# A tuned two-layer mixer kernel: larger input stages, no value products in between, and grouped rank products

## The chip, the cores and the metric

One core of one Trainium2 chip runs the kernel. The metric is the device time of one execution in microseconds; lower is better. A profile comes from one profiled execution.

## The reference

A model of two layers works on 256 tokens `x` and 256 context tokens `ctx`, each of width 2048, in float32. Cut to what matters here, the first layer begins with

```python
sh, sc, gt = modulation(c, w_ada[0], b_ada[0], 3)        # silu(c) @ w_ada + b_ada, in three parts
u  = x * (1.0 + sc) + sh
uc = ctx * (1.0 + sc_c) + sh_c                           # with the modulation of c_ctx
k, v, rf, rb, q, gate_b, a_b, a_c, a_x, gate_a = split_cols(u @ w_in_e, E_SIZES)
# the context needs k, v and the gate ranks rf, rb alone
```

Keys and values are 1024 columns each, and the ranks `rf` and `rb` 16 each. Gated linear attention, a short convolution branch, an output projection and a layer norm follow. The second layer pools, multiplies by a gate and projects. The gate vector `gt` of both layers and the scale and shift of the second come from `w_ada` as well.

## The kernel before, in words

All weights are fp32 and are read once. A weight tile is split on the chip into a rounded high part (`wh`, a cast on ScalarE, line 153) and a remainder (`wl`, a subtraction on VectorE, line 154). The modulated input is split in the same way. A product is then three matmuls: high by high, high by remainder and remainder by high (`mm3`, lines 189 to 193). Products of 128 tokens with 512 columns accumulate over the contraction tiles in a PSUM bank; there are 16 contraction tiles of 128 channels.

The first stretch of the kernel makes the modulated input `u` and the keys together, in stages over the contraction tiles. `STAGES` (line 58) lists how many tiles each stage has: 1, 1 and then seven stages of 2. For a stage of n tiles, `stage_u` (line 362)

- loads the tiles of `x` and `ctx` (`load_xc`, line 208);
- multiplies silu of the conditioning vectors with the scale and shift columns of these n tiles, over the whole contraction of `w_ada` (`mod_rows`, line 264). The weights come as 1 MiB loads, each n * 128 columns wide; four contraction tiles are summed side by side in four groups of 32 partitions (line 275);
- turns the sums into per-channel columns (`to_cols`, line 284: a copy to `arow`, then matmuls to `adaT`), adds the biases, transposes the input tiles (`px`, lines 386 and 387), applies scale and shift, and splits the result;
- when a quad of four tiles is complete, multiplies it with the 32 rank columns of the weights (`pr`, line 402).

`stage_k` (line 411) then multiplies the n tiles with two blocks of 512 key columns for four token tiles, and adds the sums to `knat` (line 420 for the first stage, line 422 for later ones). In the loop at line 563 the program first calls `w_ahead`, which issues loads and splits of the previous stage's key weights, then `stage_u` of this stage, then `stage_k` of the previous one. After the keys of 2, 4, 6 and 8 tiles, `FILLS` (line 40) adds a part of the values: `v_fill` (line 439) multiplies two contraction tiles with value columns 0 to 511 for four token tiles. The partial sums go to `vnat` (lines 451 and 453). Their split weights lie in general slots (`swh`, `swl`).

The framework schedules each engine's instructions by a model of their durations, with the program's order (shifted by `prio`) as the priority; on the chip each engine then works through its list in order. All weight loads are issued on SP's queue (line 139) in order. They take turns in four raw buffers of 1 MiB each, shared by modulation weights and all other weights, and the split parts take turns in four `wh` and four `wl` buffers of two contraction tiles each. Four PSUM banks serve the accumulations and four all else.

After the keys, 32 transposes turn them round (`nT`, line 681). The values follow, two blocks of 512 columns in units of four contraction tiles (lines 762 to 776), where `V_Q` leaves out the quads that the fills have done. Behind each unit `tick` issues some background work: the decays of the attention, and steps of the remaining modulation sums on VectorE (`aacc`, line 530), three steps a unit in this block. The other blocks of the first layer, the output projection and the second layer come after that and are not touched.

Of the kernel before, what the change touches and what calls it, by code (L numbers as in the profile page):

```python
# [9 lines left out]
F32 = mybir.dt.float32  # L10
# [3 lines left out]
ALU = mybir.AluOpType  # L14
# [3 lines left out]
P = 128  # L18
# [5 lines left out]
EPS = 1e-5  # L24
# [8 lines left out]
ADA_0 = {}  # L33
# [7 lines left out]
FILLS = {2: [(0, 0, 2)], 4: [(0, 2, 2)], 6: [(0, 4, 2)], 8: [(0, 6, 2)]}  # L41
FILL_PRIO = 0
# [15 lines left out]
STAGES = (1, 1, 2, 2, 2, 2, 2, 2, 2)  # L58
# [3 lines left out]
def kernel(  # L62
# [96 lines left out]
    # units in the order of their use; loads and splits run ahead of the products  # L159
# [71 lines left out]
    # columns 2, 3: silu of c and c_ctx; a window of 32 columns puts them on the rows 0, 1 or 2, 3 of a product  # L231
# [5 lines left out]
    # columns of colT: see the rows above  # L237
# [26 lines left out]
    def mod_rows(k0, n):  # L264
        """scale (rows 0, 1 of each group of 32) and shift (rows 2, 3) of n channel tiles, summed over every fourth contraction tile"""
        nw = n * P
        ps = mp([P, nw], "ada")
        nk = 2048 // nw
        for half, c0 in ((0, D + k0 * P), (1, k0 * P)):
            for kk in range(0, KT, nk):  # L270
                r = load_unit(w_ada[0], kk, nk, c0, nw)
                for j in range(nk):
                    kt = kk + j
                    g = kt % 4
                    nc.tensor.matmul(  # L275
                        out=ps[32 * g : 32 * g + 32, :], lhsT=sil[:, kt, 2 - 2 * half : 34 - 2 * half], rhs=r[:, j, :],
                        start=half == 0 and kt < 4, stop=half == 1 and kt >= KT - 4,
                    )
        return ps
# [38 lines left out]
    for n in STAGES:  # L318
        for nb in range(2):
            specs.append((W_E, k0, n, nb * 512))  # L320
        k0 += n
        for nb, kt, nk in FILLS.get(k0, ()):
            specs.append((W_E, kt, nk, 1024 + nb * 512))
            wide.add(len(specs) - 1)
# [10 lines left out]

    filled = [[kt + j for f in FILLS.values() for nb, kt, nk in f if nb == n for j in range(nk)] for n in range(2)]
    V_Q = [[q for q in range(4) if 4 * q not in filled[n]] for n in range(2)]
    for nb in range(2):
        block(W_E, 1024 + nb * 512, V_Q[nb])
# [22 lines left out]
    def stage_u(k0, n):  # L362
        w, n0 = n * P, k0 * P
        xc = xcs.pop(k0, None)
        if xc is None:
            xc = load_xc(k0, n)
        xs, cs = xc[:, 0:2, :], xc[:, 2:4, :]
# [11 lines left out]
        for j in range(n):  # L379
            kt = k0 + j  # L380
            if kt % 2 == 0:
                quad_u.append(slot([P, 2, 512], F32, "u"))
            u = quad_u[-1]
            px = mp([P, 512], "px")
            for t in range(2):
                nc.tensor.transpose(out=px[:, t * P : (t + 1) * P], in_=xs[:, t, j * P : (j + 1) * P], identity=ident)
                nc.tensor.transpose(out=px[:, 256 + t * P : 256 + (t + 1) * P], in_=cs[:, t, j * P : (j + 1) * P], identity=ident)
            ux, uc = u[:, kt % 2, 0:256], u[:, kt % 2, 256:512]
            nc.scalar.activation(ux, px[:, 0:256], AF.Identity, bias=shT[:, kt, 0:1], scale=scT[:, kt, 0:1])
            nc.vector.tensor_scalar(  # L390
                out=uc, in0=px[:, 256:512], scalar1=scT[:, kt, 1:2], scalar2=shT[:, kt, 1:2], op0=ALU.mult, op1=ALU.add
            )
            q, i = kt // 4, kt % 4
            nc.scalar.copy(uxh[q][:, i, :], ux)
            nc.scalar.copy(uch[q][:, i, :], uc)
            nc.vector.tensor_tensor(out=uxl[q][:, i, :], in0=ux, in1=uxh[q][:, i, :].bitcast(F32), op=ALU.subtract)
            nc.vector.tensor_tensor(out=ucl[q][:, i, :], in0=uc, in1=uch[q][:, i, :].bitcast(F32), op=ALU.subtract)
            if i == 3:
                pr = mp([P, 512], "pr")
                for g in range(4):  # L400
                    kk = kt - 3 + g
                    nc.tensor.matmul(  # L402
                        out=pr[32 * g : 32 * g + 32, :], lhsT=wr[:, kk, :], rhs=quad_u[kk // 2][:, kk % 2, :],
                        start=True, stop=True,
                    )
                if q == 0:
                    nc.vector.tensor_copy(r_acc, pr)
                else:
                    nc.vector.tensor_tensor(out=r_acc, in0=pr, in1=r_acc, op=ALU.add)
# [27 lines left out]
    vnat = []  # L437

    def v_fill(nb, kt, nk):
        """a part of the values' contraction, for the gaps that the loads leave"""  # L440
        parts = w_next((W_E, kt, nk, 1024 + nb * 512), 0, 0)
        if not vnat:
            vnat.extend(slot([P, 1024], F32, "vnat") for _ in range(4))
        with prio(FILL_PRIO):
            for m in range(4):
                acc = acc_bank("vfill")
                for j in range(nk):
                    mm3(acc, utile(m, kt + j), parts[j], j == 0, j == nk - 1)
                dst = vnat[m][:, nb * 512 : (nb + 1) * 512]
                if kt == filled[nb][0]:  # L450
                    nc.scalar.copy(dst, acc)
                else:
                    nc.vector.tensor_tensor(out=dst, in0=acc, in1=dst, op=ALU.add)

# [20 lines left out]
    def ada_unit(layer, k0, n0):  # L475
        """four contraction tiles of the modulation's weights, two slots of two"""
# [26 lines left out]
    def ada_rows_gen(layer, dst, engs):  # L503
        """the gate of a layer, on every partition: products on DVE, the sum over the channels with ones"""
# [27 lines left out]
    def ada_cols_gen(layer, n0, dst, bias, one, engs, on_pe=()):  # L532
        """a section as channel columns: products on DVE, or on PE for the column blocks in on_pe"""
# [29 lines left out]
    for n in STAGES:  # L563
        if prev:
            w_ahead(2, SPLIT_0)
        stage_u(k0, n)
        if prev:
            stage_k(*prev)
            pump_ada(ADA_0.get(sum(prev), 0))
            for f in FILLS.get(sum(prev), ()):  # L570
                v_fill(*f)
        elif SPLIT_0:
            with tc.issue_after(arow_ins[0].ins):
                w_ahead(2, 2)
        prev = (k0, n)
        k0 += n
# [45 lines left out]
    def gemm_by_tile(groups, getu, done, budget=0.0, between=None, halves=False):  # L622
        """one token tile behind the other: the first one's sums are done while the second is at work"""
# [21 lines left out]
    # masks over (key j, query i) of a block of 32: m <= (j xor i) < 2 m  # L645
# [28 lines left out]
    def to_channels(nat, dst, use_act):  # L674
        """nat: two token tiles with 128 * n columns; dst(ct) for pairs of channel tiles"""
# [88 lines left out]
    if not vnat:  # L764
        vnat.extend(slot([P, 1024], F32, "vnat") for _ in range(4))
    gg = gate_gen()
    bg.append(gg)
    for nb in range(2):
        accs = [acc_bank("vacc") for _ in range(4)]
        gemm(W_E, 1024 + nb * 512, V_Q[nb], range(4), utile, accs, budget=B_V)  # L770
        for m in range(4):
            dst = vnat[m][:, nb * 512 : (nb + 1) * 512]
            if len(V_Q[nb]) < 4:
                nc.vector.tensor_tensor(out=dst, in0=accs[m], in1=dst, op=ALU.add)
            else:
                nc.scalar.copy(dst, accs[m])
# [21 lines left out]
    def gla_gen(hp):  # L798
# [19 lines left out]
        def scores(xk, xq, flip=0):  # L818
            """keys of a block of 32 against the queries of the same block, or of its neighbour"""
# [52 lines left out]
        # chunk of 64 against the next one, tile of 128 against the other  # L872
# [108 lines left out]
    def rsqrt_act(v):  # L981
        """1 / sqrt(v + EPS): logarithm and exponential, then a Newton step"""
# [8 lines left out]
    def rsqrt(v, scale):  # L991
        """1 / sqrt(scale * v + EPS) on DVE: a seed from the exponent bits, then Newton steps"""
# [75 lines left out]
    def ln_blocks(src, order, getu, res, gt, budget, after, before=None, between=None, halves=False):  # L1068
        """sums of residual and projection and their statistics; after(m, tiles, mean, variance) when token tile m is done"""
# [265 lines left out]
```

## Time and profile before

| | |
|---|---|
| time, median of 3 runs | 1018.31 us (1013.9, 1018.31 and 1018.49) |
| profiled execution, span | 1014.8 us (no other time of this execution is listed) |
| TensorE (PE) busy | 973.4 us, 96% of the span |
| VectorE (DVE) busy | 801.4 us, 79% |
| ScalarE (ACT) busy | 463.3 us, 46% |
| DMA moved | 255.45 MB, mean 252 GB/s |

The span is what the profiler recorded from the first to the last instruction. Matmuls are pipelined: one starts while the one before is still draining, so start times tell more than durations, and a busy share near 100% doesn't mean that PE was at its peak. In tables by window, PE, PEld (weight loads into PE), DVE, ACT and POOL show their busy microseconds and the number of instructions; then come the granted PE clock, the busy share of the DMA engines and the rate.

### The profile page before, as it was taken

How to read it: one execution, taken by the hardware profiler on the slowest of the kernel's cores; microseconds unless marked ns; L12 is line 12 of the kernel's file. 1: busy time of each engine (PE TensorE's matmuls, PEld its weight loads, DVE VectorE, ACT ScalarE, POOL GpSimd, SP SyncE). 2: the span in 40 equal slices, each digit the busy share in tenths (PEclk: the TensorE clock that was granted, in tenths of full speed). 3: DMA queues.
4: the chain of work that ended last, by engine and by line, in shares of the span. 5: the costliest groups of instructions: out<-in, count | busy, mean ns of one | idle time of the engine just before them, and what ended most of it. 6: DMA issues, size and time to landing. Idle time of an engine off the chain costs nothing.

```text
span 1014.8 us, 14425 instructions
## 1 busy us (share of the span) xinstructions
PE 973.4 (96%) x5718; PEld 768.6 (76%) x5718; DVE 801.4 (79%) x1161; ACT 463.3 (46%) x629; POOL 24.0 (2%) x55
## 2 busy tenths in 40 slices
PE   5899999999999999989999999999999999999995
PEld 4566666778878877877878788887888887778885
DVE  1555556989996999699999879987769968576676
ACT  2422214365684775336563444446554454454340
POOL 2000000000000000000000000000100001000000
PEclk9999999999999999999999999999999999999998
DMA  9987899667786676757767897984887888877532
GB/s 264 327 264 261 284 289 331 203 226 254 249 298 243 199 258 219 258 171 249 245 213 248 290 322 253 323 315 170 292 308 233 277 267 277 284 268 257 175 121 83
DMA packets 150373, 255.45 MB, mean 252 GB/s; under 512 B 5079, under 2 KB 46721, under 8 KB 150305
## 3 DMA queue, kind: packets, MB, share of 16 engines
q1 hardware_dynamic: 146592, 245.13, 72.3%
q0 software_dynamic: 2896, 8.72, 2.7%
q8 instruction: 45, 0.74, 0.3%
q10 hardware_dynamic: 816, 0.68, 0.3%
q14 instruction: 24, 0.19, 0.0%
HBM read 252.41 MB, written 2.10 MB: 251 GB/s over the span
## 4 chain that ended last, share of the span: by engine, by line
PE 43%; DVE 31%; DMA 19%; issue 4%; ACT 3%; SPq 0%; DVEq 0%; ACTq 0%
DMA raw<-in_w_ada_dram 16%; DVE wl L154 11%; DVE aacc L530 8%; PE oacc L191 5%; PE oacc L193 5%; PE oacc L192 5%; PE xacc L193 4%; PE xacc L192 4%; PE xacc L191 4%; PE ada L275 2%; PE kacc L191 2%; PE kacc L193 2%; PE kacc L192 2%; PE pr L402 1%; DMA raw<-in_w_in_e_dram 1%
## 5 line engine op out<-in xcount | busy, mean ns | idle before, releaser
L153 ACT CAST wh<-raw 128x1024 fp32r<-128x1024 f32 (+1 forms) x250 | 257.8, 1044 | 252.6 <-PE xacc L193 97.8
L154 DVE TENSOR_TENSOR wl<-raw,wh 128x1024 fp32r<-128x1024 f32 (+1 forms) x250 | 297.9, 1211 | 40.6 <-ACT wh L153 38.1
L530 DVE SCALAR_TENSOR_TENSOR aacc<-raw,sil,aacc 128x512 f32<-128x512 f32 x240 | 179.5, 748 | 42.6 <-DMA raw<-in_w_ada_dram 38.7
L191 PE MATMUL xacc<-wh,uxh 128*128 128x512 f32 x384 | 152.6, 397 | 0.0
L193 PE MATMUL xacc<-wh,uxl 128*128 128x512 f32 x384 | 151.8, 395 | 0.0
L192 PE MATMUL xacc<-wl,uxh 128*128 128x512 f32 x384 | 150.3, 391 | 0.1
L192 PE MATMUL xacc<-wl,u1h 128*128 128x512 f32 x240 | 94.4, 393 | 3.2 <-DVE wl L154 3.0
L191 PE MATMUL xacc<-wh,u1h 128*128 128x512 f32 x240 | 95.2, 397 | 0.8 <-ACT u1h L1156 0.8
L193 PE MATMUL xacc<-wh,u1l 128*128 128x512 f32 x240 | 93.7, 391 | 0.0
L192 PEld LDWEIGHTS xacc<-wl,uxh 128*128 128x128 f32 x384 | 72.1, 188 | 16.2 <-DVE wl L154 1.0
L193 PEld LDWEIGHTS xacc<-wh,uxl 128*128 128x128 f32 x384 | 72.2, 188 | 15.3 <-issue 0.2
L191 PEld LDWEIGHTS xacc<-wh,uxh 128*128 128x128 f32 x384 | 72.1, 188 | 15.5 <-ACT wh L153 0.5
L422 DVE TENSOR_TENSOR knat<-kacc,knat 128x512 f32<-128x512 f32 x64 | 42.8, 686 | 34.5 <-PE kacc L193 34.3
L192 PEld LDWEIGHTS xacc<-wl,u1h 128*128 128x128 f32 x240 | 45.1, 188 | 16.0 <-DVE wl L154 6.1
L191 PEld LDWEIGHTS xacc<-wh,u1h 128*128 128x128 f32 x240 | 45.1, 188 | 11.2 <-ACT u1h L1156 1.3
L193 PEld LDWEIGHTS xacc<-wh,u1l 128*128 128x128 f32 x240 | 45.1, 188 | 9.5 <-DVE u1l L1157 0.4
L286 ACT COPY arow<-ada 128x256 f32<-128x256 f32 (+1 forms) x9 | 3.1, 349 | 100.8 <-PE ada L275 100.8
L275 PE MATMUL ada<-raw,sil 128*32 128x256 f32 (+1 forms) x576 | 36.4, 382 | 10.8 <-DMA raw<-in_w_ada_dram 10.7
L191 PE MATMUL oacc<-wh,y1h 128*128 128x512 f32 (+1 forms) x120 | 45.5, 379 | 0.0
L193 PE MATMUL oacc<-wh,y1l 128*128 128x512 f32 (+1 forms) x120 | 45.0, 375 | 0.0
L192 PE MATMUL oacc<-wl,y1h 128*128 128x512 f32 (+1 forms) x120 | 45.0, 375 | 0.0
L275 PEld LDWEIGHTS ada<-raw,sil 128*32 128x32 f32 x576 | 17.3, 119 | 27.4 <-issue 12.6
(326 smaller groups left out, 1685.6 us busy)
## 6 DMA issues: line engine op xcount, KB each, us to landing
raw<-in_w_ada_dram SPq DMA_DIRECT2D x96, 1024.0 KB, 6.4
raw<-in_w_in_e_dram SPq DMA_DIRECT2D x54, 1024.0 KB, 5.7
raw<-in_w_in_o_dram SPq DMA_DIRECT2D x32, 1024.0 KB, 6.5
raw<-in_w_out_e_dram SPq DMA_DIRECT2D x16, 1024.0 KB, 7.0
raw<-in_w_out_o_dram SPq DMA_DIRECT2D x16, 1024.0 KB, 5.2
raw<-in_w_in_e_dram SPq DMA_DIRECT2D x18, 512.0 KB, 6.9
raw<-in_w_pool_dram SPq DMA_DIRECT2D x4, 1024.0 KB, 8.1
gt<-in_b_ada_dram POOLq DMA_DIRECT2D x8, 256.0 KB, 4.6
```

What stands on the lines that cost most here:

```text
L153: nc.scalar.copy(h, r[:, j : j + w, :])
L154: nc.vector.tensor_tensor(out=l, in0=r[:, j : j + w, :], in1=h.bitcast(F32), op=ALU.subtract)
L191: nc.tensor.matmul(out=acc, lhsT=uh, rhs=wh, start=start, stop=False)
L192: nc.tensor.matmul(out=acc, lhsT=uh, rhs=wl, start=False, stop=False)
L193: nc.tensor.matmul(out=acc, lhsT=ul, rhs=wh, start=False, stop=stop)
L275: nc.tensor.matmul(out=ps[32 * g : 32 * g + 32, :], lhsT=sil[:, kt, 2 - 2 * half : 34 - 2 * half], rhs=r[:, j, :], start=half == 0 and kt ...
L286: arow_ins.append(nc.scalar.copy(a[:, :nw], ps))
L402: nc.tensor.matmul(out=pr[32 * g : 32 * g + 32, :], lhsT=wr[:, kk, :], rhs=quad_u[kk // 2][:, kk % 2, :], start=True, stop=True,)
L422: nc.vector.tensor_tensor(out=dst, in0=acc, in1=dst, op=ALU.add)
L530: e.scalar_tensor_tensor(out=a, in0=r[j], scalar=sc, in1=a, op0=ALU.mult, op1=ALU.add)
```

## The change

- The stages are 1, 1, 2, 4, 4 and 4 tiles. In the stages of four tiles the modulation weights are 512 columns wide (four contraction tiles a load instead of eight), and the key weights come as 1 MiB loads of four tiles instead of 0.5 MiB loads of two. The key products accumulate over four tiles before they are added to `knat`. The input is still loaded in pairs of tiles.
- `FILLS` and `v_fill` are gone; the values' blocks are computed whole, and copied from PSUM by ScalarE.
- The four rank products of a quad are issued as a group with a higher priority: the last one first, and the others behind it.

```diff
-FILLS = {2: [(0, 0, 2)], 4: [(0, 2, 2)], 6: [(0, 4, 2)], 8: [(0, 6, 2)]}
-FILL_PRIO = 0
+PR_PRIO = 200
...
-STAGES = (1, 1, 2, 2, 2, 2, 2, 2, 2)
+STAGES = (1, 1, 2, 4, 4, 4)
...
-        for nb, kt, nk in FILLS.get(k0, ()):
-            specs.append((W_E, kt, nk, 1024 + nb * 512))
-            wide.add(len(specs) - 1)
...
-        block(W_E, 1024 + nb * 512, V_Q[nb])
+        block(W_E, 1024 + nb * 512)
...
     def stage_u(k0, n):
-        w, n0 = n * P, k0 * P
-        xc = xcs.pop(k0, None)
-        if xc is None:
-            xc = load_xc(k0, n)
-        xs, cs = xc[:, 0:2, :], xc[:, 2:4, :]
+        w = n * P
+        pairs = [(k, min(2, k0 + n - k)) for k in range(k0, k0 + n, 2)]
+        xts = [xcs.pop(k, None) for k, _ in pairs]
+        xts = [load_xc(*h) if t is None else t for t, h in zip(xts, pairs)]
...
-            for t in range(2):
-                nc.tensor.transpose(out=px[:, t * P : (t + 1) * P], in_=xs[:, t, j * P : (j + 1) * P], identity=ident)
-                nc.tensor.transpose(out=px[:, 256 + t * P : 256 + (t + 1) * P], in_=cs[:, t, j * P : (j + 1) * P], identity=ident)
+            xc, c0 = xts[j // 2], (j % 2) * P
+            for t in range(4):
+                nc.tensor.transpose(out=px[:, t * P : (t + 1) * P], in_=xc[:, t, c0 : c0 + P], identity=ident)
...
             if i == 3:
-                pr = mp([P, 512], "pr")
-                for g in range(4):
-                    kk = kt - 3 + g
-                    nc.tensor.matmul(
-                        out=pr[32 * g : 32 * g + 32, :], lhsT=wr[:, kk, :], rhs=quad_u[kk // 2][:, kk % 2, :],
-                        start=True, stop=True,
-                    )
...
+                ranks(kt)
+
+    def ranks(kt):
+
+        pr = mp([P, 512], "pr")
+
+        def product(g):
+            kk = kt - 3 + g
+            return nc.tensor.matmul(
+                out=pr[32 * g : 32 * g + 32, :], lhsT=wr[:, kk, :], rhs=quad_u[kk // 2][:, kk % 2, :], start=True, stop=True)
+
+        with prio(-PR_PRIO):
+            first = product(3)
+            with tc.issue_after(first.ins):
+                for g in range(3):
+                    product(g)
...
-            pump_ada(ADA_0.get(sum(prev), 0))
-            for f in FILLS.get(sum(prev), ()):
-                v_fill(*f)
...
-        gemm(W_E, 1024 + nb * 512, V_Q[nb], range(4), utile, accs, budget=B_V)
+        gemm(W_E, 1024 + nb * 512, range(4), range(4), utile, accs, budget=B_V)
         for m in range(4):
-            dst = vnat[m][:, nb * 512 : (nb + 1) * 512]
-            if len(V_Q[nb]) < 4:
-                nc.vector.tensor_tensor(out=dst, in0=accs[m], in1=dst, op=ALU.add)
-            else:
-                nc.scalar.copy(dst, accs[m])
+            nc.scalar.copy(vnat[m][:, nb * 512 : (nb + 1) * 512], accs[m])
```

The definition of `v_fill` goes with its callers. `ADA_0` was empty, so its removal changes nothing.

## Rows read from the trace of the kernel before

**Rows 1.** The page, part 1: busy us, share of the span, instructions.
```profile
PE 973.4 (96%) x5718; PEld 768.6 (76%) x5718; DVE 801.4 (79%) x1161; ACT 463.3 (46%) x629; POOL 24.0 (2%) x55
```

**Rows 2.** Windows: stretch, its length, engines, PEclk, DMA share, GB/s.
```profile
0.00:24.00 24.00, 12.82 (x119) 9.47 (x120) 4.01 (x14) 6.11 (x12) 7.04 (x17) 1.00 1.02 259
24.00:33.39 9.39, 8.95 (x80) 5.97 (x79) 5.47 (x12) 4.82 (x11) 0.00 (x0) 1.00 1.09 349
33.39:42.00 8.61, 6.24 (x68) 3.69 (x65) 2.58 (x6) 0.37 (x1) 0.00 (x0) 1.00 1.01 340
124.30:144.80 20.50, 20.34 (x136) 12.13 (x136) 10.92 (x20) 4.50 (x9) 0.00 (x0) 1.00 0.93 304
144.80:161.50 16.70, 16.70 (x125) 11.81 (x124) 10.09 (x15) 4.10 (x5) 0.00 (x0) 1.00 1.05 287
198.00:270.00 72.00, 71.70 (x326) 58.88 (x323) 65.80 (x96) 42.35 (x65) 0.51 (x5) 1.00 0.75 260
```

**Rows 3.** Timeline of PE, 130 to 145 us: start, us, engine, line, operation.
```profile
130.22 0.39 PE L193 MATMUL kacc<-wh,uxl 128*128 128x512 f32 x1
...
131.88 0.39 PE L192 MATMUL kacc<-wl,uch 128*128 128x512 f32 x1
...
139.23 0.40 PE L191 MATMUL kacc<-wh,uxh 128*128 128x512 f32 x1
...
144.46 0.39 PE L193 MATMUL kacc<-wh,ucl 128*128 128x512 f32 x1
```

**Rows 4.** Timeline of PE, a stage's small work and a quad's rank products.
```profile
132.34 0.51 PE L289 MATMUL adaT<-sel,arow 128*128 128x4 f32 x4
132.71 0.30 PE L386 MATMUL px<-ident,xc 128*128 128x128 f32 x1
...
133.71 1.05 PE L402 MATMUL pr<-u,wr_acc 128*32 128x512 f32 x4
134.69 0.50 PE L191 MATMUL kacc<-wh,uch 128*128 128x512 f32 x1
...
135.58 1.04 PE L402 MATMUL pr<-u,wr_acc 128*32 128x512 f32 x2
```

**Rows 5.** The fills' tile: ns min/median/max, first and last start; one of six groups.
```profile
L191 PE MATMUL vfill<-swh,uxh x16: 389/389/499, 44.5 to 120.8; 128*128 128x512 f32 x16
```

**Rows 6.** Timeline of SP's queue, and the window (columns as in rows 2) where these loads land.
```profile
163.73 13.81 SPq L139 DMA_DIRECT2D raw<-in_w_in_e_dram  x5
...
170.00:175.00 5.00, 5.00 (x25) 2.19 (x23) 1.60 (x6) 3.67 (x8) 0.20 (x1) 1.00 1.04 386
```

**Rows 7.** Timeline of PE, the second stage's last unit and its first key product.
```profile
24.52 1.08 PE L275 MATMUL ada<-raw,sil 128*32 128x128 f32 x32
...
28.71 0.50 PE L191 MATMUL kacc<-wh,uxh 128*128 128x512 f32 x1 [0.44 <-ACT uxh L394]
```

**Rows 8.** Timeline of PE, end of the keys and start of the values.
```profile
194.20 0.39 PE L193 MATMUL kacc<-wh,ucl 128*128 128x512 f32 x1
...
198.09 0.48 PE L191 MATMUL vacc<-wh,uxh 128*128 128x512 f32 x1
```

**Rows 9.** Timeline of PE, where matmuls are far apart and where close.
```profile
17.71 0.63 PE L192 MATMUL kacc<-wl,uxh 128*128 128x512 f32 x1
...
18.14 0.63 PE L191 MATMUL kacc<-wh,uxh 128*128 128x512 f32 x1
...
22.81 0.39 PE L191 MATMUL kacc<-wh,uch 128*128 128x512 f32 x1
...
23.05 0.39 PE L192 MATMUL kacc<-wl,uch 128*128 128x512 f32 x1
...
39.62 1.07 PE L275 MATMUL ada<-raw,sil 128*32 128x256 f32 x16 [1.88 <-DMA raw<-in_w_ada_dram]
...
45.76 0.39 PE L193 MATMUL vfill<-swh,uxl 128*128 128x512 f32 x1
...
45.98 0.39 PE L191 MATMUL vfill<-swh,uxh 128*128 128x512 f32 x1
```

More of the change, by code (lines that the diff above doesn't have):

```diff
@@ L32 @@
 GW_AT = 12
-ADA_0 = {}
 ADA_ORDER = "cgh"
@@ L334, in widen @@
         wide.update(range(len(specs) - n, len(specs)))
-    filled = [[kt + j for f in FILLS.values() for nb, kt, nk in f if nb == n for j in range(nk)] for n in range(2)]
-    V_Q = [[q for q in range(4) if 4 * q not in filled[n]] for n in range(2)]
     for nb in range(2):
-        block(W_E, 1024 + nb * 512, V_Q[nb])
+        block(W_E, 1024 + nb * 512)
     for nb in range(2):
@@ L398, in stage_u @@
             if i == 3:
-                pr = mp([P, 512], "pr")
-                for g in range(4):
-                    kk = kt - 3 + g
-                    nc.tensor.matmul(
-                        out=pr[32 * g : 32 * g + 32, :], lhsT=wr[:, kk, :], rhs=quad_u[kk // 2][:, kk % 2, :],
-                        start=True, stop=True,
-                    )
-                if q == 0:
-                    nc.vector.tensor_copy(r_acc, pr)
-                else:
-                    nc.vector.tensor_tensor(out=r_acc, in0=pr, in1=r_acc, op=ALU.add)
+                ranks(kt)
[10 more added lines that the diff above has]
+                    product(g)
+        if kt == 3:
+            nc.vector.tensor_copy(r_acc, pr)
+        else:
+            nc.vector.tensor_tensor(out=r_acc, in0=pr, in1=r_acc, op=ALU.add)
     def stage_k(k0, n):
@@ L435, in gate_weights @@
             wps.append(wp)
[L437 to L448, printed above, removed]
-                dst = vnat[m][:, nb * 512 : (nb + 1) * 512]
[L450 to L453, printed above, removed]
     ones = const([P, P], F32, "ones")
@@ L763 @@
         pass
-    if not vnat:
-        vnat.extend(slot([P, 1024], F32, "vnat") for _ in range(4))
+    vnat = [slot([P, 1024], F32, "vnat") for _ in range(4)]
     gg = gate_gen()
@@ L769 @@
         accs = [acc_bank("vacc") for _ in range(4)]
-        gemm(W_E, 1024 + nb * 512, V_Q[nb], range(4), utile, accs, budget=B_V)
+        gemm(W_E, 1024 + nb * 512, range(4), range(4), utile, accs, budget=B_V)
         for m in range(4):
-            dst = vnat[m][:, nb * 512 : (nb + 1) * 512]
-            if len(V_Q[nb]) < 4:
-                nc.vector.tensor_tensor(out=dst, in0=accs[m], in1=dst, op=ALU.add)
-            else:
-                nc.scalar.copy(dst, accs[m])
+            nc.scalar.copy(vnat[m][:, nb * 512 : (nb + 1) * 512], accs[m])
     qT = [slot([P, 4, SEQ], F32, "qT") for _ in range(2)]
```

## The prediction

> **What bounds the kernel now.** The page comes first: TensorE (PE) is busy for 96% of the span, VectorE (DVE) for 79% [rows 1]. Busy time of pipelined matmuls proves little, so the second view is the windows, cut at the borders of the input stages [rows 2]. Up to 42 us PE has holes (12.82 of 24, 8.95 of 9.39, 6.24 of 8.61 us busy) and the DMA share is at or above 1: the loads bound the start, at 349 and 340 GB/s. From 124 to 161 us PE is full, and less is moved (304 and 287 GB/s): there PE bounds. The third view, the timeline, shows that this PE is really full: 24 key matmuls from 139.23 to 144.46 us, 0.2275 us each [rows 3]. So the kernel is a queue of PE work behind a start that is bound by loads, and the change is worth what it takes out of that queue, less the holes that it makes.
>
> **What the change moves.** I write "unit" for 1 MiB of modulation weights; there are 32 in the first layer before and after, so SP issues as many of these. Four SP loads of 0.5 MiB (the value weights of the fills) leave the first stretch and come back as two of 1 MiB in the values' block. Per contraction tile the first stretch loads two units, 0.5 MiB of key weights and 0.25 MiB of input.
>
> Prices per instruction:
> - A key or value matmul: 0.2275 us [rows 3].
> - A unit between key matmuls: from 130.22 to 131.88 us are 1.66 us, with one unit and one more key matmul between the two shown; less two plain steps that is 1.2 us [rows 3]. A unit 512 wide has the same columns in fewer matmuls; I price it alike.
> - A stage's own small PE work: from 132.34 to 133.71 us are 1.4 us for two tiles, of which eight transposes take 1.0 [rows 4]. For four tiles 2.4 us.
> - Rank products: two together take 0.98 us until the next matmul starts, and one alone lasts as long as the two (1.04 and 1.05 us) [rows 4]. So products that run together cost as one. A quad has three such bursts now; as one group it has one, 1.2 us with the change of shape on both sides (as for a unit).
> - The fills: six groups of 16 matmuls like the one shown, 96 in all [rows 5], 21.8 us. They don't vanish: values' columns 0 to 511 get two more weight units after the keys. PE is the bound on both sides, so I count 21.8 us out and 21.8 us in.
>
> Start of the new four-tile stages. By 42 us 12.4 MB have landed (the three first windows, rate by length) [rows 2]. To have the modulation of eight tiles takes 16.8 MB of units, 2.1 of key weights, 2.1 of input and 0.35 of small things, 21.3 MB. At which rate do the 8.9 MB left come? Units that are 256 columns wide are read in runs of 1 KB and came at 349 and 340 GB/s, mean 345. Units 512 wide are read in runs of 2 KB; the trace has this for key and value weights, of which five loads were issued from 163.73 us on, and the window from 170 to 175 us moved 386 GB/s [rows 6]. I take 386, since its loads have the shape of the new units, and keep 345 as the other end (2.7 us later). So the eight tiles' modulation is there 23.1 us after 42, at 65.1 us. PE has only two tiles' keys to do meanwhile (10.9 us), so the last unit runs as it lands (1.0 us), and 3.1 us after it the keys start, as in the second stage, whose last unit ends at 25.60 and whose first key matmul starts at 28.71 us [rows 7]: 69.2 us.
>
> From there PE has 12 tiles of 24 key matmuls, 65.5 us; 16 units, 19.2; two stages of small work, 4.8; three rank groups, 3.6: 93.1 us. The same prices applied to the kernel before, from 41.65 us on (336 key matmuls 76.4, fills 21.8, 24 units 28.8, stages 9.2, ranks 13), give 149 us, where the trace takes 152.6 up to the last key matmul's end at 194.4 [rows 8]. Some 2% is thus unpriced, waits for evictions mostly; with it 95 us, and the keys end near 164.2 us. A check from the loads' side: up to the last unit 44.8 MB are needed, 32.4 more than at 42 us, 83.9 us at 386, so 125.9; then 1.0, 3.1, 21.8 of keys and 1.2 of ranks end at 153. Even at 345 that is 163, so PE decides.
>
> Keys end at 164.2 in place of 194.4 us: 30.2 us. Given back: 21.8 us of values. **Sum: 8.4 us faster.**
>
> Costed at nothing: 24 fewer key evictions, 12 fill additions and the smaller splits. They lie on DVE, which is off the bound in the first stretch; a stage's evictions stand behind the same PE work. In the values' block DVE is busy 65.80 of 72 us [rows 2]; two more units bring two more background steps there, 21.8 us of PE to lay them beside, and 6.2 us of idle DVE per block as cover. If that were not enough, DVE's work would still not be more in sum, only earlier, and what it holds up in this block it has done before the next. I put 0 to 3 us on that and take 0. What lies between the last key and the first value matmul (3.9 us [rows 8]) stays as it is.
>
> The profiled execution has a span of 1014.8 us, 3.5 below the median of 1018.31; no other time of its own is shown. The sum is worked out on that span (1006.4) and carried over to the median: **1009.9 us**, 0.8% faster. A measurement of this kernel can tell about 0.5% (5.1 us) from no change.
>
> **The rivals.**
>
> (a) *Waits at the start of the four-tile stages eat the gain.* With four tiles the key weights come as two units of 1 MiB that are queued behind the modulation, so the first lands some 3 us (1 MiB at 345 to 386 GB/s) and the second 6 us after it, and has yet to be split on ScalarE and DVE, which at that time also make four tiles of input. There are no fills now for PE to do meanwhile. That is 0 to 4 us at 65 us. The third rank group may also not come together: the order only asks that the last product goes first, and PE, in order, waits for its input; up to 1.1 us a quad. With loads nearer to 345 GB/s (2.7 us) that makes 4 to 9 us: 1014 to 1019, no change that can be told.
>
> (b) *PE falls to its lower clock in the wait.* At the start key matmuls are 0.43 us apart (17.71, 18.14), 512 columns at 1.2 GHz, after PE had waited for loads; the granted clock column says 1.00 there, so it doesn't show this. But after the wait of 1.88 us ahead of the unit at 39.62 us the matmuls at 45.76 and 45.98 are 0.22 us apart, the upper level, 2.4 GHz [rows 9]. New waits are of that kind: a unit lands every 2.7 to 3.0 us and takes 1.0. At the start the lower level was gone by 22.81 and 23.05; from 17.71 on that is 5.1 us, in which half the speed was lost, so a repeat costs 2.6 us: 1012.5. The Trainium skill says in TensorE: Matmul & The Clock Gate, HAM oscillation — how this bites in real kernels, that a wait for DMA between bursts of matmuls sends PE back to the lower clock, so that every burst begins slow; by that rule this rival would be the forecast, and the wait at 39.62 us doesn't bear it out.
>
> (c) *Slower: the loads don't keep their rate.* Weights and modulation share four raw buffers in turn. A four-tile stage puts two of them under key weights until these are split, and a split needs the split buffers of the stage before, all four of which a four-tile stage fills. In that time only two buffers take units. If the rate falls to 295 GB/s, the mean of the two windows without fills [rows 2], the last unit lands at 42 + 109.6 = 151.6 us, the keys end 27.1 later at 178.7, and with 21.8 of values that is 6.1 us over 194.4: 1024.4. It decides from a last unit after 145.5 us, below 313 GB/s. For it: in neither of these windows was the rate above that. Against it: in them the runs were shorter, and PE was full and, in order, held the buffers until it came to the units; in the wait for the eight tiles it takes each unit as it lands, as it did in the windows at 349 and 340.
>
> (d) *More gain:* the unpriced 2% (1.9 us) goes with the evictions, and what is left of the third stage's keys covers the 3.1 us ahead of the fourth's: 1004.9.
>
> **How the numbers follow.** The forecast 0.38, (d) 0.09, (b) 0.07: these are faster by over 0.5%, together 0.54. (a) 0.29, no change. (c) 0.17, slower. (a) is the heaviest rival because the late key weights come of the order of the loads, and only their cover is open. (c) is left out of the range. The range takes in the others: up to (a)'s 1019 with 2 of the 3 us put on DVE above, 1021; down to (d) less most of the 4.4 us by which the fastest of the three runs (1013.9) lies under the median, 1001.
>
> **What would show it.** Key matmuls end near 164 us, the last modulation unit runs on PE near 135 to 143, and the values' block lasts some 94 us (now 72, from 198 to 270 us). Eight rank records run in one burst, four bursts in all. DMA stays over 340 GB/s from 25 to 65 us and is at times idle later. PE has some 5 us of holes between 42 and 69 us (27 us with 10.9 of keys, 9.6 of units and 1.4 of small work), and nearly none later. Key matmuls near 69 us that are 0.43 us apart would show (b); a rate under 313 GB/s and a last unit after 145.5 us would show (c). The prediction is wrong if the keys end after 172.6 us, or if the values' block grows by more than 25 us: then PE was not the bound there.

## The result and the profile after

The changed kernel is **slower** by 1.1%: 1029.38 us, median of four runs (1027.14 to 1029.81), against 1018.4 us for the kernel before (four runs, 1013.9 to 1018.72). The ratio is 1.0106, with a 95% interval from 1.0083 to 1.0128. The forecast was 1009.9 us and its range ended at 1021. The profiled execution took 1029.81 us with a span of 1027.9 us, 13.1 us over the span before.

The page after: part 1 (as [rows 1]) and the granted clock in 40 slices, in tenths:

```profile
PE 974.3 (95%) x5526; PEld 767.8 (75%) x5526; DVE 776.4 (76%) x1115; ACT 468.5 (46%) x628; POOL 24.0 (2%) x55
...
PEclk9978999998999999999999999999999999999998
```

PE issues 192 instructions fewer and is busy for as long as before: 24 units of 16 matmul instructions have become 24 of 8 with the same columns. PEclk says where to look: the third and fourth slice (7 and 8, from 51 to 103 us) and the tenth (8, from 231 to 257 us).

The windows after, cut at the last unit and the first key matmul of each four-tile stage, with the values' block as the last line (columns as in [rows 2]):

```profile
24.00:42.00 18.00, 15.22 (x146) 9.85 (x146) 8.38 (x18) 5.88 (x13) 0.00 (x0) 1.00 1.08 358
42.00:60.00 18.00, 17.03 (x94) 10.10 (x95) 10.78 (x19) 3.12 (x7) 0.00 (x0) 1.00 1.05 375
60.00:68.80 8.80, 5.25 (x36) 0.65 (x28) 0.16 (x1) 0.00 (x0) 0.00 (x0) 0.83 1.04 388
68.80:78.60 9.80, 7.33 (x36) 5.18 (x32) 5.30 (x14) 6.44 (x15) 0.00 (x0) 0.50 1.06 376
78.60:111.30 32.70, 32.70 (x161) 19.43 (x157) 9.70 (x13) 2.40 (x3) 0.00 (x0) 0.93 0.86 282
111.30:118.80 7.50, 4.82 (x40) 3.50 (x36) 5.18 (x14) 5.60 (x14) 0.00 (x0) 1.00 0.95 335
118.80:149.10 30.30, 30.22 (x153) 17.27 (x153) 14.51 (x17) 5.22 (x6) 0.41 (x2) 1.00 0.90 295
149.10:154.90 5.80, 4.52 (x35) 3.83 (x31) 2.50 (x6) 3.83 (x7) 0.00 (x0) 1.00 0.92 338
154.90:178.60 23.70, 23.59 (x105) 17.89 (x106) 21.23 (x46) 8.27 (x14) 0.00 (x0) 1.00 0.55 178
...
181.40:287.40 106.00, 102.02 (x445) 82.61 (x444) 92.78 (x137) 59.91 (x92) 1.81 (x9) 0.95 0.75 252
```

After its last unit, each four-tile stage has a stretch in which PE does hardly any keys: 9.8, 7.5 and 5.8 us, with none, three and seven key matmuls started in it. Between these stretches PE is full. The values' block lasts 106.0 us, where the kernel before has this window, with 115 PE instructions fewer:

```profile
198.10:270.50 72.40, 72.10 (x330) 59.28 (x327) 66.19 (x96) 42.75 (x66) 0.51 (x5) 1.00 0.75 260
```

The timeline after, PE and one line of ScalarE at the first four-tile stage, then PE at the start of the second one, the last unit, the end of the keys and the start of the values (as [rows 4, 7 to 9]; in brackets the idle time before, and what ended it):

```profile
64.25 1.06 PE L273 MATMUL ada<-raw,sil 128*32 128x512 f32 x8 [1.63 <-DMA raw<-in_w_ada_dram]
66.96 1.94 PE L273 MATMUL ada<-raw,sil 128*32 128x512 f32 x8 [1.64 <-DMA raw<-in_w_ada_dram]
69.60 1.87 PE L287 MATMUL adaT<-sel,arow 128*128 128x4 f32 x8 [0.70 <-ACT arow L284]
71.32 3.65 PE L379 MATMUL px<-ident,xc 128*128 128x128 f32 x16
...
76.75 1.93 PE L399 MATMUL pr<-u,wr_acc 128*32 128x512 f32 x8 [1.77 <-DVE u L382]
76.80 1.06 ACT L151 CAST wh<-raw 128x1024 fp32r<-128x1024 f32 x1
78.61 1.22 PE L189 MATMUL kacc<-wh,uxh 128*128 128x512 f32 x2
...
81.34 0.63 PE L189 MATMUL kacc<-wh,uxh 128*128 128x512 f32 x1
81.77 0.63 PE L190 MATMUL kacc<-wl,uxh 128*128 128x512 f32 x1
...
112.30 0.95 PE L287 MATMUL adaT<-sel,arow 128*128 128x4 f32 x8
113.11 1.94 PE L379 MATMUL px<-ident,xc 128*128 128x128 f32 x16
117.68 1.06 PE L399 MATMUL pr<-u,wr_acc 128*32 128x512 f32 x8 [2.63 <-DVE u L382]
118.83 0.74 PE L189 MATMUL kacc<-wh,uxh 128*128 128x512 f32 x2
...
148.14 1.06 PE L273 MATMUL ada<-raw,sil 128*32 128x512 f32 x8
...
178.36 0.39 PE L191 MATMUL kacc<-wh,ucl 128*128 128x512 f32 x1
...
181.43 0.48 PE L189 MATMUL vacc<-wh,uxh 128*128 128x512 f32 x1
```

The first value matmul starts 16.7 us earlier than before (181.43 against 198.09 [rows 8]), the values' block is 33.5 us longer (105.9 against 72.4 us, from its first matmul to that of the next block), and what follows is 3.8 us shorter: −16.7 + 33.5 − 3.8 = +13.0, the change of span but for rounding. The forecast had −30.2, +21.8 and 0. So both halves of the exchange went wrong (the keys end 14.4 us later than forecast, of which 0.8 us came back between the last key and the first value; the block grew by 11.7 us more), each by more than the whole gain that was forecast, 8.4 us.

### The profile page after: what moved, and what is told of

It is laid out like the page before. It is cut to its first block, busy times and chain, and to the rows that moved or that the text cites. A ratio compares the mean times of both kernels' runs of the same rounds, so it can differ in the third digit from the quotient of the medians.

```text
span 1027.9 us, 13957 instructions
## 1 busy us (share of the span) xinstructions
PE 974.3 (95%) x5526; PEld 767.8 (75%) x5526; DVE 776.4 (76%) x1115; ACT 468.5 (46%) x628; POOL 24.0 (2%) x55
## 4 chain that ended last, share of the span: by engine, by line
PE 57%; DVE 20%; DMA 15%; issue 4%; ACT 3%; SPq 0%; DVEq 0%; ACTq 0%
DMA raw<-in_w_ada_dram 14%; DVE wl L152 7%; PE xacc L189 6%; PE oacc L189 6%; PE xacc L191 6%; PE xacc L190 6%; PE oacc L191 6%; PE oacc L190 6%; DVE aacc L513 5%; PE ada L273 3%; PE vacc L189 3%; PE vacc L190 3%; PE vacc L191 3%; PE kacc L191 2%; PE kacc L189 2%
## 5 line engine op out<-in xcount | busy, mean ns | idle before, releaser
L151 ACT CAST wh<-raw 128x1024 fp32r<-128x1024 f32 (+1 forms) x254 | 262.9, 1045 | 270.7 <-PE xacc L191 106.4
L152 DVE TENSOR_TENSOR wl<-raw,wh 128x1024 fp32r<-128x1024 f32 (+1 forms) x254 | 303.1, 1212 | 62.1 <-ACT wh L151 58.5
L190 PEld LDWEIGHTS xacc<-wl,uxh 128*128 128x128 f32 x384 | 72.4, 189 | 17.1 <-DVE wl L152 1.7
L423 DVE TENSOR_TENSOR knat<-kacc,knat 128x512 f32<-128x512 f32 x40 | 27.2, 688 | 42.5 <-PE kacc L191 42.3
L273 PE MATMUL ada<-raw,sil 128*32 128x512 f32 (+2 forms) x384 | 36.8, 495 | 12.8 <-DMA raw<-in_w_ada_dram 12.8
L284 ACT COPY arow<-ada 128x512 f32<-128x512 f32 (+2 forms) x6 | 2.7, 443 | 82.7 <-PE ada L273 82.7
L273 PEld LDWEIGHTS ada<-raw,sil 128*32 128x32 f32 x384 | 10.4, 121 | 27.5 <-issue 14.7
```

The lines of the kernel that those rows point to most:

```text
L151: nc.scalar.copy(h, r[:, j : j + w, :])
L152: nc.vector.tensor_tensor(out=l, in0=r[:, j : j + w, :], in1=h.bitcast(F32), op=ALU.subtract)
L190: nc.tensor.matmul(out=acc, lhsT=uh, rhs=wl, start=False, stop=False)
L273: nc.tensor.matmul(out=ps[32 * g : 32 * g + 32, :], lhsT=sil[:, kt, 2 - 2 * half : 34 - 2 * half], rhs=r[:, j, :], start=half == 0 and kt ...
L284: arow_ins.append(nc.scalar.copy(a[:, :nw], ps))
```

## The experiments

All times are medians of at least four runs, and ratios are to the kernel before, run beside on the same chip (its medians were 1017.74, 1017.4 and 1017.71 us). "Keys" is the start of the last key matmul, "block" the time from the first value matmul to the first one of the next block, both from the timeline.

| kernel | time, us | ratio, 95% interval | keys | block |
|---|---|---|---|---|
| before | 1018.4 | 1 | 194.2 | 72.4 |
| after | 1029.38 | 1.0106 (1.0083 to 1.0128) | 178.4 | 105.9 |
| e1_ranks_alone | 1006.57 | 0.9902 (0.9872 to 0.9932) | 184.3 | 72.7 |
| e2_ranks_apart | 1031.92 | 1.0143 (1.0110 to 1.0176) | 183.0 | 102.7 |
| e3_values_by_dve | 1028.92 | 1.0106 (1.0078 to 1.0133) | 180.1 | 104.7 |
| e4_stages_of_two | 1025.43 | 1.0088 (1.0062 to 1.0113) | 175.7 | 106.0 |
| e5_splits_first | 1026.63 | 1.0102 (1.0058 to 1.0146) | 178.8 | 103.6 |
| e6_fill_waits | 1009.39 | 0.9915 (0.9885 to 0.9946) | 191.7 | 72.6 |
| e7_warm_thrown | 1031.00 | 1.0129 (1.0103 to 1.0156) | 183.2 | 103.0 |
| e9_values_less_background | 1023.29 | 1.0054 (1.0031 to 1.0076) | 176.9 | 100.3 |
| e10_values_no_modulation | 1069.48 | 1.0498 (1.0468 to 1.0527) | 179.1 | 97.9 |
| e11_ranks_and_splits | 1010.45 | 0.9926 (0.9903 to 0.9948) | 187.9 | 72.9 |

The block column sorts the table by itself: it is 73 us wherever fills make a part of the values, and 98 to 106 us wherever the block makes all of them, whatever else is done. It also shows how far single profiles differ: with the same code for the block and all of the values in it, e2, e5, e7, e4 and the changed kernel have 102.7 to 106.0 us.

### The rank group alone, and the change without it

e1_ranks_alone puts only the group into the kernel before; e2_ranks_apart takes only the group out of the changed kernel.

```diff
             if i == 3:
-                pr = mp([P, 512], "pr")
-                for g in range(4):
-                    ...
+                ranks(kt)
```

> The kernel before with one part of the change: a quad's rank products as one group. Theory A (the group itself is a gain, as priced: four groups of 1.2 us in place of some 13 us of bursts, stages of two tiles leave other keys to cover its wait): 6 to 8 us faster, 1010 to 1013. Theory B (the group makes PE, in order, wait for the quad's last tile each time, 2.2 and 2.9 us in two of the quads of the changed kernel, and gives back what it saves): within 3 us of 1018.4.

> The changed kernel with the rank products apart, as before. If the group's wait is what holds the keys up at 74.6 and 114.8 us (5 us together), the time falls by 3 to 6 us, to 1023 to 1026. If the keys would have to wait there anyway, because ScalarE splits their weights (76.80 us) only after four tiles of input, the bursts come back for nothing: 3 to 8 us slower than the changed kernel, 1032 to 1037.

Measured: the group alone makes the kernel before 1% faster, 11.2 us between the medians and so more than the 6 to 8 us of theory A, and the last key matmul starts 9.9 us earlier. Taken out of the changed kernel, it leaves the time at 1031.92 us, 2.5 us more, an interval that overlaps the changed kernel's. So the group is the good part of the change, though with the larger stages and no fills hardly any of its gain can be told; and its waits of 1.77 and 2.63 us above are not what made the change slow. What is slow must cost some 23 us (1029.38 − 1006.57).

### The larger stages undone, the fills still gone

```diff
-STAGES = (1, 1, 2, 4, 4, 4)
+STAGES = (1, 1, 2, 2, 2, 2, 2, 2, 2)
```

> The changed kernel with the stages of before: 1, 1 and seven of 2; still no fills, ranks grouped. If the size of the stages is the cause (no keys left over to cover the way from the last modulation unit to the first key, 10.8 and 7.5 us), the keys end near 165 us in place of 178.6 and the time falls by 10 to 13 us, to 1016 to 1019. If the lack of fills is the cause, the waits and the lower clock stay: 1026 to 1031.

Measured: 1025.43 us, only 4 us under the changed kernel. Beside e1 this kernel differs by the missing fills and what follows from them (values computed whole, copied from PSUM by ScalarE), and it is 18.9 us slower. The two windows of each tell how: from 24 us to the end of the keys, and the values' block, first of e1, then of e4 (columns as above):

```profile
24.00:184.70 160.70, 155.69 (x1062) 110.56 (x1055) 101.96 (x182) 46.98 (x86) 0.41 (x2) 0.98 0.92 300
188.20:261.00 72.80, 72.17 (x330) 59.33 (x328) 66.85 (x98) 42.95 (x66) 0.52 (x5) 1.00 0.74 252
```

```profile
24.00:176.10 152.10, 140.68 (x979) 93.06 (x978) 92.09 (x171) 41.87 (x80) 0.37 (x2) 0.97 0.94 303
179.60:285.60 106.00, 100.94 (x437) 82.21 (x436) 94.82 (x140) 58.84 (x91) 1.83 (x9) 0.95 0.77 261
```

The fills are 96 matmuls, 21.8 us at the price of the prediction. Without them PE is busy for 15.0 us less (155.69 − 140.68) and idle for 6.4 us more (11.4 against 5.0 us), so the keys end only 8.6 us earlier. What PE waits for in this stretch, first in e1, then in e4 (engine, line, what it waited for, us in total, times, longest):

```profile
PE ada L276 <- DMA raw<-in_w_ada_dram: 3.3, 3, 1.9
...
PE kacc L192 <- ACT uxh L395: 0.5, 1, 0.5
```

```profile
PE ada L273 <- DMA raw<-in_w_ada_dram: 4.9, 3, 2.6
PE kacc L189 <- ACT uxh L386: 3.9, 6, 1.0
PE kacc L189 <- DVE knat L423: 1.4, 2, 1.0
PE kacc L189 <- ACT uch L387: 0.7, 2, 0.4
```

Most of the new idle time, 4.1 us, is waiting for ScalarE's casts of the input at the start of a stage; 1.6 us are for units and 1.4 us for additions to `knat` (and 0.7 us of waiting for a fill's weights is gone). By these waits the fills covered the way from a stage's last unit to its first key more than they covered loads. The loads follow close behind, though: from 60 to 80 us the DMA share rises from 0.75 to 0.93 without the fills, as these windows of e1 and of e4 show:

```profile
60.00:80.00 20.00, 20.00 (x127) 14.35 (x126) 12.74 (x23) 5.45 (x10) 0.00 (x0) 1.00 0.75 248
```

```profile
60.00:80.00 20.00, 19.14 (x143) 12.29 (x143) 10.88 (x19) 4.55 (x10) 0.00 (x0) 1.00 0.93 307
```

The other 6.8 us, between 21.8 and 15.0, are in the key matmuls: counted from start to start in the trace, with idle time left out, they take 88.7 us in e1 and 96.9 in e4. Some 3.5 us of that is the lower clock, at which they ran for 7.1 us; the rest is units and short waits between them, not told apart.

The values' block takes 33.2 us more, not 21.8. The difference of the two, 24.6 us, is the difference of these two spans (1026.8 and 1002.2 us). They belong to the fastest run of e1 and the slowest of e4; between the medians it is 18.9 us.

### The fills given back to the larger stages

```diff
+FILLS = {2: [(0, 0, 2)], 4: [(0, 2, 2)], 8: [(0, 4, 4)]}
...
+            for f in FILLS.get(sum(prev), ()):
+                v_fill(*f)
```

with `v_fill`, its loads and `V_Q` as in the kernel before.

> The changed kernel with the fills back, behind the keys of 2, 4 and 8 tiles (the same 96 matmuls as before, stages of 1, 1, 2, 4, 4, 4, ranks grouped). If the fills were nearly free because they filled waits, as the kernel before with grouped ranks says against the same stages without fills, the keys end some 8 us later than 178.6 and the values' block takes 73 us in place of 106: 1029.4 + 8 - 33, 1002 to 1007. If the large stages themselves cost (the way through ScalarE and VectorE from the last unit to the first key, with the rank group ahead of the fill), 1011 to 1018.

Measured: 1009.39 us, 20 us under the changed kernel and between the two forecasts. The keys end 13.3 us later and the block is 33.3 us shorter, 72.6 us as before. This is the same exchange seen from the other end. Beside e1 the larger stages bring nothing: 2.8 us more between the medians, with intervals that overlap.

### Work thrown into the waits

Two of the fills are added to the changed kernel and their sums are not used; the values are computed whole as well. All that is needed is still computed.

```diff
+FILLS = {2: [(0, 0, 2)], 4: [(0, 2, 2)]}
...
+                dst = drop[m][:, nb * 512 : (nb + 1) * 512]
+                nc.scalar.copy(dst, acc)
```

> The changed kernel with 48 value matmuls added in the waits behind the keys of 2 and 4 tiles, whose results are thrown away (the values' block computes all of the values as well): 10.9 us of PE work and 1 MiB of loads more. If PE waits there anyway and pays for it with the lower clock from 66 to 83 us, the added work is nearly free: 1026 to 1032, with no lower clock there. If PE is full, it costs what it takes: 1037 to 1041.

Windows of e7 around the wait at 60 us:

```profile
60.00:70.00 10.00, 9.83 (x58) 4.87 (x56) 3.46 (x5) 0.00 (x0) 0.00 (x0) 1.00 1.04 386
70.00:84.00 14.00, 9.90 (x47) 6.34 (x44) 6.57 (x16) 7.72 (x16) 0.00 (x0) 0.64 0.91 317
```

Forty-eight matmuls (10.9 us) more on PE and 1 MiB more to load cost 1.6 us between the medians, within the intervals. By pushing the keys back they fill PE from 60 to 70 us (9.83 of 10, where the changed kernel had 5.25 of 8.8), and the clock holds there, but in the chain of small work behind, from 70 us on, PE has holes and the clock is down as before (0.64). So in the whole time most of this work was free, though the keys end 4.8 us later (183.2 us); the block, 2.9 us shorter here, is within the spread of single profiles. Keeping PE busy up to 70 us does not cure the start of the stage.

### The start of a stage: splits first

```diff
-SPLIT_PRIO0 = 0
+SPLIT_PRIO0 = 300
```

> The changed kernel with the key weights' splits scheduled ahead of the input's work in the first stretch. If the keys of a four-tile stage start late (78.6 and 118.8 us) because ScalarE casts their weights only behind four tiles of input, they start 2 to 3 us earlier in each of three stages: 4 to 8 us less than the changed kernel, 1021 to 1025. If the rank group, which needs the last of the four tiles, holds PE there anyway: no change, 1027 to 1031.

> The kernel before with grouped ranks and, in addition, the first stretch's splits scheduled ahead of the input's work. If late splits hold the keys up in stages of two tiles as well, 2 to 5 us less than with grouped ranks alone (1006.6): 1002 to 1005. If the fills cover that already: 1005 to 1009.

In the changed kernel ScalarE casts the key weights at 76.80 us, behind its work on four tiles of input. e5 puts the splits ahead in the changed kernel, e11 does so in e1. Measured: 1026.63 us, not distinguishable from the changed kernel, and 1010.45 us, not better than e1. In e5 the first four-tile stage starts its keys 8.29 us after the start of its last unit (70.51 to 78.80 us), in place of 11.65 us; but that unit comes 3.55 us later, after a stretch with the clock down (0.73 from 42 to 60 us), and the last key matmul starts no earlier, at 178.8 us. PE's waits moved to the cast of the input (1.14, 1.99 and 1.98 us for `uxh`). So another order of this work brings no gain that can be told; whether its amount is what delays the keys was not tried.

### The longer values' block

Why does it take 33.5 us more for 96 more matmuls? The timeline of PE after, where it waits inside the block:

```profile
199.03 0.80 PE L699 MATMUL pz<-rp,wp 96*128 96x512 f32 x1 [2.04 <-DVE rp L683]
...
236.40 1.77 PE L699 MATMUL pz<-rp,wp 96*128 96x512 f32 x3 [1.19 <-DVE scT L292]
...
238.79 0.79 PE L189 MATMUL vacc<-wh,uxh 128*128 128x512 f32 x1 [0.63 <-ACT vnat L751]
...
240.24 0.63 PE L189 MATMUL vacc<-wh,uxh 128*128 128x512 f32 x1
240.66 0.63 PE L190 MATMUL vacc<-wl,uxh 128*128 128x512 f32 x1
...
287.37 0.39 PE L189 MATMUL xacc<-wh,uxh 128*128 128x512 f32 x1
```

and the windows behind two of these waits:

```profile
198.90:202.30 3.40, 3.27 (x8) 2.60 (x9) 0.89 (x3) 2.38 (x6) 0.00 (x0) 0.51 1.04 395
...
236.50:243.30 6.80, 6.17 (x14) 4.17 (x15) 6.66 (x10) 4.64 (x9) 0.03 (x1) 0.50 0.81 270
```

The background work that `tick` issues behind every unit has small products on PE (`pz` for the decays). PE works in order, so a product whose input VectorE or ScalarE has not finished holds all value matmuls behind it. Then the clock is down: value matmuls are 0.42 us apart (240.24, 240.66) in place of 0.2275. Three experiments change what else is done in the block. e3 copies the values by VectorE; e9 issues three quarters of the background (modulation steps and decays); e10 none of the modulation steps.

```diff
-            nc.scalar.copy(vnat[m][:, nb * 512 : (nb + 1) * 512], accs[m])
+            nc.vector.tensor_copy(vnat[m][:, nb * 512 : (nb + 1) * 512], accs[m])
```

```diff
-ADA_V = 3
+ADA_V = 2.25
...
-B_V = 4500
+B_V = 3375
```

```diff
-ADA_V = 3
+ADA_V = 0
```

> The changed kernel, with the values' sums copied from PSUM by VectorE in place of ScalarE. If the hole of 5.3 us between the two value blocks (233.45 to 238.79 us) and the lower clock behind it come of the copy that stands behind the decays' work on ScalarE, the time falls by 5 to 8 us, to 1021 to 1024. If VectorE is as far behind there (23.37 of 25 us busy), the hole stays: 1027 to 1031.

> The changed kernel with a quarter less background work behind each unit of the values (2.25 modulation steps for 3, and a credit of 3375 for 4500), so that eight units issue what six did before. If the values' block is 11 us longer than its matmuls say because two more units brought more background than PE's time covers, it takes 95 to 99 us in place of 106 and the kernel 1021 to 1025. If that background is only paid later: 1027 to 1031.

> The changed kernel with no modulation steps behind the units of the values (0 for 3); the decays stay. If these steps are what makes the values' block 106 us long (they hold VectorE and the raw buffers, and the decays' products and the weights' splits come late), the block takes 91 to 95 us, some 12 less, and the kernel 1015 to 1022 or, if the steps must be paid in full later, as before, 1027 to 1031. If the decays alone cause the waits, the block stays above 100 us.

Measured: e3 changes nothing (1028.92 us), and the waits for `rp` and `scT` stay. e9 shortens the block by 5.6 us, 2.4 us below the lowest of the profiles above, and the time by 6 us, with intervals that do not meet. e10 shortens it by 8.0 us, to 97.9, between its two forecasts and with 2.3 us of waits of the decays' products still in it, and pays for it later with 40 us (1069.48 us), as a window and PE's waits in it show:

```profile
692.00:735.00 43.00, 9.80 (x35) 7.96 (x34) 36.00 (x53) 6.29 (x7) 0.00 (x0) 0.54 0.89 303
```

```profile
PE adaS L534 <- DVE aacc L513: 32.7, 3, 11.7
```

The modulation sums, put off, come due all together before the output of the first layer, where PE has 9.80 us of work in 43 and nothing to lay beside it. So the background has to be done somewhere; but two more units with their ticks are more than this block hides. Counted from start to start in the two traces, the block splits up like this:

| us | before | after | more |
|---|---|---|---|
| value matmuls (288 and 384) | 66.3 | 91.9 | 25.6 |
| small products | 5.8 | 10.0 | 4.2 |
| PE idle | 0.3 | 4.0 | 3.7 |
| block | 72.4 | 105.9 | 33.5 |

At 0.2275 us the 96 matmuls more would take 21.8 us. Most of the 3.8 us above that is the lower clock: in the two windows at 0.50 PE was busy for 9.4 us, where the same work takes half as long at the upper level, so 4.7 us went there, some 3.5 of them in value matmuls.

## Why the prediction was wrong

**The step that failed** is "PE is the bound on both sides, so I count 21.8 us out and 21.8 us in". Neither side held.

- *Out.* The fills' work is not worth its price to the queue. When it is taken away, PE waits at the starts of the stages, more for ScalarE and VectorE than for loads, loses speed in the keys, and has the loads close behind it: 8.6 us of 21.8 show at the end of the keys (e1 against e4), 13.3 with the larger stages (after against e6). The prediction read PE's fullness off 124 to 161 us [rows 2], in windows that hold no fills, and took it for the places where the fills stood. PE was full there too, with the fills in it (from 60 to 80 us 20.00 us in e1, 19.14 in e4 without them); and a full window doesn't say what comes up behind it when work is taken out.
- *In.* The block grew by 33.5 us, not 21.8. The text itself named this mark: over 25 us, "then PE was not the bound there". The term "0 to 3 us on that and take 0" measured 11.7 us: 4.2 of small products that two more units bring to PE itself, 3.7 of waits, 3.8 of slower value matmuls, mostly the lower clock. DVE's idle time was counted as cover, and DVE does have more of it now (92.78 of 106 us busy); but PE, in order, waits for single results of DVE and ScalarE, as for `rp` and `scT` above.

The larger stages by themselves brought neither gain nor loss that can be told (e6 against e1 2.8 us, after against e4 4 us, both slower, with intervals that overlap). By the prediction's own prices the group was worth 8.2 us of its 8.4; that term came true and more, and the loss is the exchange of the fills, 18.9 us (e4 against e1) to 20 us (after against e6). Where the stages missed their own numbers follows.

**Keys end near 164.2 us: 178.6.** First step: keys start at 78.61, not 69.2 us, 9.4 late. The unit came 1.9 us later than 65.1 (66.96), and from its start to the first key matmul are 11.65 us, where the prediction had 1.0 + 3.1. That 3.1 was read off a stage of one tile [rows 7] and applied to four: two bursts of small work that last 1.87 and 3.65 us, the wait for `u` of the last tile (1.77), the weights' cast behind. Second step: the later starts took 7.5 and 5.8 us (with three and seven key matmuls in them), priced 3.6 each. From 78.6 to 178.6 are 100 us, for which the prediction had 95.

**Rival (a)**, waits at the start of the stages, is what happened there, and was too small: 4 to 9 us, where the first start alone lost 9.4.

**Rival (b)**, the lower clock, was given 0.07 and did happen: after waits of 1.63 and 1.64 us for units the granted clock was 0.50, the lower of the two levels, and key matmuls are 0.43 us apart at 81.34 and 81.77, the mark that was named. The clock was down over this window and up in the next:

```profile
65.80:82.90 17.10, 13.47 (x50) 8.81 (x51) 9.60 (x19) 8.84 (x17) 0.00 (x0) 0.50 0.85 297
82.90:111.30 28.40, 28.40 (x148) 16.00 (x147) 5.39 (x8) 0.00 (x0) 0.00 (x0) 1.00 0.96 316
```

The 2.6 us that it was priced at covers little more than what the keys alone lost from 78.6 to 82.9 us (half of 4.3, so 2.2); the small work before them was slower too. From the first product for `adaT` to the first key are 9.01 us (69.60 to 78.61) and at the second four-tile stage, at the upper level, 6.53 us (112.30 to 118.83). With the last unit's burst (1.94 us, 1.06 for others) and the keys that makes some 5.5 us for the lower clock, an estimate from these rows. One wait of 1.88 us without such an effect [rows 9] was taken for a rule. The Trainium skill (TensorE: Matmul & The Clock Gate, HAM oscillation — how this bites in real kernels) has waits for DMA between bursts send PE back to the lower clock. The trace of the changed kernel agrees with it (0.50 from 65.8 us). The waits in the page's example are longer than 1.64 us, though, so it doesn't by itself make this rival the forecast, as the prediction has it.

**Rival (c)**, loads that lose their rate, has the right sign, and met some of its marks: the last unit starts at 148.14 us (151.6, deciding from 145.5), and the keys end at 178.6 (178.7). The rate that was to fall under 313 GB/s did not: the windows from 42 to 149.1 us make 322 on the mean. Nor was its cause met. While PE waits, the loads come at 388 GB/s (60 to 68.8 us), as the prediction took them, and the rate falls to 282 and 295 only where PE is full, from 78.6 to 111.3 and from 118.8 to 149.1 us. The late end comes of the starts.

**Right** was the rank group: priced at 13 us less four times 1.2, so 8.2 us, and measured as 9.9 us at the keys' end and 11.2 in the whole (e1); in the changed kernel it is 2.5 us (e2), not told from nothing. Right too was the rate of the loads with 2 KB runs (386 taken; 375 measured from 42 to 60 us, 388 to 68.8). That DVE's work done earlier is gone later would fit the 3.8 us gained behind the block; it was not tried by itself.

**Open** stays what the lower clock costs by experiment: no kernel here removes it and nothing else, and the 5.5 and 4.7 us are estimates from rows. Of the block's excess the shares of decays and modulation were only narrowed by e9 and e10. e6 against e1 is within the intervals. The best kernel of these is e1, the kernel before with the grouped rank products and nothing else, ahead of both.

## What to carry to other kernels

Work that makes an engine look full may be covering waits of that engine. It is then not worth its price when it is taken out, and can cost its price and more where it is put back. Before moving it, ask what the engine would wait for in its place (loads, and results of other engines), and read the window where the work stands, not one beside it. Price the start of a stage by the chain that runs in series (sums, columns, transposes, casts, splits), and let it grow with the tiles of the stage. A change of several parts is best run part by part: here the one that looked smallest carried the whole gain.

## What was not expected of the hardware

The last wait alone doesn't tell whether the clock falls. In the kernel before, a wait of 1.88 us ahead of the unit at 39.62 us left matmuls 0.22 us apart [rows 9]. In e1, whose code is the same up to the ranks, a wait of 1.93 us at the same place was followed by 6.8 us at the lower level. What came before differs: in the kernel before two units ran together ahead of the wait, in e1 a further wait of 0.75 us stood between them. The kernel before, then e1 and its window:

```profile
35.66 2.08 PE L275 MATMUL ada<-raw,sil 128*32 128x256 f32 x32
```

```profile
36.54 1.07 PE L276 MATMUL ada<-raw,sil 128*32 128x256 f32 x16 [0.75 <-DMA raw<-in_w_ada_dram]
39.54 1.07 PE L276 MATMUL ada<-raw,sil 128*32 128x256 f32 x16 [1.93 <-DMA raw<-in_w_ada_dram]
```

```profile
40.70:47.50 6.80, 5.67 (x19) 4.69 (x20) 3.64 (x8) 4.74 (x9) 0.00 (x0) 0.50 0.66 211
```

Whether the wait of 0.75 us made the difference is not shown. One such wait in one trace settles nothing, and a forecast with waits of this size has to carry both cases.
